# Order of the plain tiles and of the activation sums in two SwiGLU gate stages

## The chip, the cores and the metric

One core of one Trainium2 chip. The metric is the device time of one execution in microseconds, the median over runs. TensorE (PE) multiplies, VectorE (DVE), ScalarE (ACT) and GpSimd (POOL) do the element work, and SyncE (SP) issues most DMA transfers.

## The reference, cut to what matters

```python
def _rmsnorm(x, g):
    xf = x.astype(jnp.float32)
    y = xf * lax.rsqrt(jnp.mean(xf * xf, axis=-1, keepdims=True) + NORM_EPS)
    return (y * g.astype(jnp.float32)).astype(x.dtype)

def _swiglu(h, w_gate, w_up, w_down):
    return (jax.nn.silu(h @ w_gate) * (h @ w_up)) @ w_down
```

The block is a feed-forward net (FFN1), three parallel mixers with an output projection, a second feed-forward net (FFN2) and a final norm. x is 1024 x 1024, the hidden width is 2816, everything is float32. The change touches only the two gate stages, `silu(h @ w_gate) * (h @ w_up)` with h = rmsnorm(x).

## The kernel before, in words

Activations lie transposed: 8 tiles of 128 features (k = 0..7), each in two halves of 512 tokens. Float32 precision is kept by splitting each operand into a high and a low part (`split`, L96 to L102): ScalarE makes the high part (L99), VectorE or GpSimd the low part by a subtraction (L102). Each product is then three matmuls (`mm3`, L119 high x high, L120 high x low of h, L121 low of the weight x high of h).

A gate stage (class `Gates`) has 22 tiles of the hidden width. The first four, f = 0..3, are plain (`plain`, L326): per tile two weights (gate and up, `gu`) in two pieces each, both halves of the tokens, 48 matmuls per half. Tiles 0 and 1 load their weights once for each half. The other 18 are done in pairs by a seven-product block scheme (`run`): h is seen as a 2 x 2 matrix of blocks (k = 0..3 or 4..7, half 0 or 1), and for each k = 0..3 `sums` (L342) forms four combinations t1 to t4 of the four blocks, and splits each: three subtractions on GpSimd (L349, L350, L352), one on VectorE (L351), and then t1, t2, t4, t3. They overwrite the normalized tiles. t4 goes into the slots of h's half 1, k = 0..3, which the plain tiles read last. A weight in flight has one of 4 pairs of high and low tiles (`whi`, `wlo`) and one of 8 raw tiles (`wraw`); the slot comes free with its last reader.

FFN1 starts with the norm still unknown: f = 0, 1 are first run for half 0 on the unnormalized tiles `hu` (scaled by the norm's gain), and `finish` (L308) multiplies by the reciprocal root r afterwards (L313, L323). Meanwhile `step` computes r of both halves and splits the normalized half 1. After that f = 0, 1 run for half 1, then half 0 is normalized (L182) and split, and f = 2, 3 run on both halves.

In FFN2 half 0 of h comes out of the output projection (`wout`) while half 1 is still being projected; the normalized tiles of half 0 are stored to DRAM (`xnd`, L1663), since their ring slots are needed, and loaded back into ring slots (L1711) for the sums after the plain tiles. `rg` is the ring of 10 slots.

The code gives the order of issue; a scheduler then moves instructions ahead within each engine's list as their operands allow. In FFN1 it already draws the sums into the time of the plain tiles. Each engine, and SyncE's DMA queue, works its list strictly in order. In the trace, `h` and `t` are split tiles (one name for high and low), `pgu` a bank of accumulated gate products, `rst` the reciprocal root, `x` half 0 of FFN1's input, `rg` also half 1.

Of the kernel before, what the change touches and what calls it, by code (L numbers as in the profile page):

```python
# [8 lines left out]
FT = mybir.dt.float32  # L9
FR = mybir.dt.float32r  # L10
# [8 lines left out]
KT = 8  # L19
HALF = 512  # L20
# [267 lines left out]
class Gates:  # L288
# [34 lines left out]
            nc.vector.tensor_mul(sg, sg, r)  # L323
        nc.sync.dma_start(self.ad[f][half], sg)

    def plain(self, fs, halves, h, r=lambda: None, loads=None, step=None):  # L326

        B = self.B
        for f in fs:
            w = [[loads.pop(0) if loads else B.wload(self.wgu[f, gu, q], 512) for q in range(2)] for gu in range(2)]  # L330
            for half in halves:
                ps = [self.bank() for _ in range(2)]
                for k in range(KT):
                    wc = slice((k % 4) * 128, (k % 4) * 128 + 128)
                    for gu in range(2):
                        B.mm3(ps[gu], [a[:, wc] for a in w[gu][k // 4]], h[half][k], k == 0, k == KT - 1)
                if step:
                    step()
                for gu in range(2):
                    self.finish(f, half, gu, ps[gu], r())  # L340

    def sums(self, k, raw):  # L342


        B, nc = self.B, self.nc
        a11, a12, a21, a22 = raw
        add = nc.gpsimd
        out = [None] * 4
        add.tensor_sub(a11, a12, a11)  # L349
        add.tensor_sub(a12, a22, a12)  # L350
        nc.vector.tensor_sub(a22, a22, a11)  # L351
        add.tensor_sub(a21, a21, a22)  # L352
        for n, a, eng in ((1, a11, "dve"), (2, a22, "dve"), (4, a21, "pool"), (3, a12, "pool")):
            pool, tag = (B.hp, lambda p: f"h{p}1{k}") if n == 4 else (self.tp, lambda p: f"t{p}{n}{k}")
            t = out[n - 1] = [pool.tile([128, HALF], FR, name=f"t{p}{n}{k}", tag=tag(p)) for p in range(2)]
            B.split(*t, a, eng_lo=eng)
        return out

    def blocks(self, m):

# [1066 lines left out]
def body(ctx, tc, A, VO):  # L1427
    nc = tc.nc
# [44 lines left out]
    with ExitStack() as fs:  # L1473
        with ExitStack() as st:
            B.more_w(fs)
            ring = ring_of(st)
            F = Gates(B, st, ring, A["wgu1"], ad)
            g1 = VO["ffn1_norm"]
            hu, h = ([], []), ([], [])

            def loadx(half, k):
                t = ring() if half else F.tp.tile([128, HALF], FT, name=f"x0{k}", tag=f"t{k // 4}3{k % 4}")
                nc.sync.dma_start(t, A["xT"][k][:, halves[half]])
                return t

            xt, early, acc, r = [[], []], [], [None, None], {}
            for k in range(KT):
                xt[0].append(loadx(0, k))
                if k in LOADS:
                    early.append(B.wload(A["wgu1"][0, LOADS[k][0], LOADS[k][1]], 512))  # L1490
            for k in range(KT):
                xt[1].append(loadx(1, k))
            for k in range(KT):
                B.split_scaled(*B.htile(hu, 0, k), xt[0][k], g1 + k)
                acc[0] = B.add_square(np_, acc[0], xt[0][k], nc.gpsimd)

            def step():
                for half in range(2):
                    if half not in r:
                        r[half] = B.rstd_tiles(np_, nps, xt[1], one) if half else B.rstd(np_, nps, acc[0])  # L1500
                        if half:
                            for k in range(KT):
                                B.normed(xt[1][k], xt[1][k], r[1], g1 + k)
                                B.split(*B.htile(h, 1, k), xt[1][k], eng_lo="pool" if k % 2 else "dve")

            F.plain((0, 1), (0,), hu, lambda: r[0], early, step)
            B.load_consts()
            F.plain((0, 1), (1,), h)
            for k in range(KT):
                B.normed(xt[0][k], xt[0][k], r[0], g1 + k)  # L1510
                B.split(*B.htile(h, 0, k), xt[0][k])
            F.plain((2, 3), (0, 1), h)
            sums = [F.sums(k, (xt[0][k], xt[1][k], xt[0][k + 4], xt[1][k + 4])) for k in range(4)]
            F.run(h, sums)
        mt = met.enter_context(tc.tile_pool(name="met", bufs=1, side="right", reuse_waits="tile"))
        xp = xs.enter_context(tc.tile_pool(name="xp", bufs=1, side="right", reuse_waits="tile"))
# [132 lines left out]
    with ExitStack() as fs:  # L1649
        np_, nps = B.norm_pool(fs)  # L1650
        B.more_w(fs)
        with ExitStack() as st:
# [31 lines left out]
            with tc.tile_pool(name="mgp", bufs=1, reuse_waits="tile") as mp, \  # L1684
# [14 lines left out]
                weave([late(), wout(0, mps)])  # L1699
                weave([wout(1, mps)])  # L1700
            F = Gates(B, st, ring, A["wgu2"], ad)
            F.plain((0, 1), (0,), h, step=lambda: B.tick(4))
            B.drain()
            F.plain((0, 1), (1,), h)
            F.plain((2, 3), (0, 1), h)
            sums = []
            for k in range(4):
                two = []
                for j in (k, k + 4):
                    t = ring()  # L1710
                    nc.sync.dma_start(t, xnd[j])  # L1711
                    two.append(t)
                sums.append(F.sums(k, (two[0], xt[1, k], two[1], xt[1, k + 4])))
            F.run(h, sums)
        xp = fs.enter_context(tc.tile_pool(name="xp2", bufs=1, side="right", reuse_waits="tile"))
        x = [xp.tile([128, S], FT, name=f"x{k}") for k in range(KT)]
# [92 lines left out]
```

## Time and profile before

| | us |
|---|---|
| median of 3 runs | 2962.35 (2958.25 to 2962.57) |
| profiled execution | 2965.43 |
| its span | 2963.4 |
| TensorE busy | 2842.6 (96%) |
| VectorE busy | 1749.2 (59%) |
| ScalarE busy | 1274.8 (43%) |
| GpSimd busy | 636.9 (21%) |

The span is the profiled part of one execution; 2.0 us lie around it. The mean granted clock of TensorE is 0.981 of full speed. FFN1's gate stage begins the program; FFN2's begins at about 2241 us. A busy share is an average over the whole span; what a wait costs is read from the stretch in which it stands.

### The profile page before, as it was taken

What the parts mean: (1) busy time and instruction counts of PE and PEld (TensorE: products, weight loads), DVE (VectorE), ACT (ScalarE), POOL (GpSimd) and SP (SyncE); (2) the same over time, 40 slices, a digit from 0 to 9 for tenths busy, and PEclk for the clock granted to TensorE, in tenths of its full rate; (3) what the DMA queues carried; (4) which work ended last, traced back from release to release, by engine and by line L of the source; (5) the groups of instructions that cost most, each with busy time, mean ns of one, the idle gap of its engine ahead of it and who ended that gap; (6) DMA issues with size and microseconds to landing.
All of it is one profiled execution on the core that took longest, in us unless ns stands there. A gap on an engine that the chain in (4) does not pass through costs nothing. (4 is left out here: it accounts for less than half of the span.)

```text
span 2963.4 us, 39951 instructions
## 1 busy us (share of the span) xinstructions
PE 2842.6 (96%) x13790; PEld 2254.4 (76%) x13790; DVE 1749.2 (59%) x3788; ACT 1274.8 (43%) x2743; POOL 636.9 (21%) x721
## 2 busy tenths in 40 slices
PE   7999999999999999999999889999999799999997
PEld 4788888887887777767767677777787588888886
DVE  8455555627466656666654367888765455555526
ACT  5333333315454345544443356666543233333313
POOL 4422220004011111111110133433321522220002
PEclk8999999999999999999999999999999899999999
DMA  4222226514323212222221642212564222225413
GB/s 150 75 85 86 82 79 202 163 35 148 96 64 87 69 56 72 64 70 73 59 67 57 183 146 80 85 59 69 182 212 140 71 78 83 82 86 191 140 41 105
DMA packets 203046, 294.40 MB, mean 99 GB/s; under 512 B 46131, under 2 KB 75707, under 8 KB 202844
## 3 DMA queue, kind: packets, MB, share of 16 engines
q1 hardware_dynamic: 186384, 263.25, 28.8%
q10 hardware_dynamic: 16460, 28.61, 3.2%
q8 instruction: 108, 1.77, 0.3%
q14 instruction: 94, 0.77, 0.1%
HBM read 223.51 MB, written 68.27 MB: 98 GB/s over the span
## 5 line engine op out<-in xcount | busy, mean ns | idle before, releaser
L99 ACT ACTIVATE whi<-wraw 128x512 fp32r<-128x512 f32 x576 | 345.1, 603 | 755.9 <-PE pgu L120 289.2
L102 DVE TENSOR_TENSOR wlo<-wraw,whi 128x512 fp32r<-128x512 f32 (+1 forms) x568 | 406.4, 719 | 383.0 <-ACT whi L99 343.4
L119 PE MATMUL mm<-h,whi 128*128 128x512 f32 x800 | 329.6, 412 | 0.2 <-ACT gbt L1543 0.2
L121 PE MATMUL mm<-h,wlo 128*128 128x512 f32 x800 | 320.1, 401 | 7.3 <-DVE wlo L102 7.3
L120 PE MATMUL mm<-h,whi 128*128 128x512 f32 x800 | 317.6, 397 | 0.0
L119 PE MATMUL pgu<-h,whi 128*128 128x512 f32 x688 | 273.2, 398 | 15.1 <-ACT whi L99 10.4
L120 PE MATMUL pgu<-h,whi 128*128 128x512 f32 x688 | 274.3, 399 | 8.5 <-DVE h L102 4.5
L121 PE MATMUL pgu<-h,wlo 128*128 128x512 f32 x688 | 274.0, 399 | 7.1 <-DVE wlo L102 7.1
L121 PE MATMUL pd<-a,wlo 128*128 128x512 f32 x704 | 274.3, 390 | 1.7 <-DVE wlo L102 1.7
L119 PE MATMUL pd<-a,whi 128*128 128x512 f32 x704 | 274.0, 389 | 0.6 <-DVE x L256 0.6
L120 PE MATMUL pd<-a,whi 128*128 128x512 f32 x704 | 273.9, 389 | 0.0
L119 PE MATMUL pgu<-t,whi 128*128 128x512 f32 x576 | 225.8, 392 | 8.7 <-ACT t L99 6.6
L120 PE MATMUL pgu<-t,whi 128*128 128x512 f32 x576 | 225.8, 392 | 8.5 <-DVE t L102 8.5
L121 PE MATMUL pgu<-t,wlo 128*128 128x512 f32 x576 | 224.9, 390 | 0.0
L132 POOL TENSOR_TENSOR acc<-acc,sq 128x512 f32<-128x512 f32 x46 | 67.5, 1467 | 579.9 <-ACT sq L131 576.8
L121 PEld LDWEIGHTS mm<-h,wlo 128*128 128x128 f32 x800 | 151.1, 189 | 40.1 <-DVE wlo L102 9.1
L119 PEld LDWEIGHTS mm<-h,whi 128*128 128x128 f32 x800 | 151.3, 189 | 36.1 <-issue 5.3
L120 PEld LDWEIGHTS mm<-h,whi 128*128 128x128 f32 x800 | 151.5, 189 | 28.5 <-issue 3.0
L119 PEld LDWEIGHTS pgu<-h,whi 128*128 128x128 f32 x688 | 131.9, 192 | 45.0 <-ACT whi L99 12.6
L120 PEld LDWEIGHTS pgu<-h,whi 128*128 128x128 f32 x688 | 131.8, 192 | 40.5 <-DVE h L102 6.0
L256 DVE SCALAR_TENSOR_TENSOR x<-pd,x 128x512 f32<-128x512 f32 x128 | 87.7, 687 | 126.2 <-PE pd L121 121.3
L121 PEld LDWEIGHTS pgu<-h,wlo 128*128 128x128 f32 x688 | 131.7, 191 | 38.5 <-DVE wlo L102 11.1
(405 smaller groups left out, 6071.9 us busy)
## 6 DMA issues: line engine op xcount, KB each, us to landing
wraw<-in_wgu SPq DMA_DIRECT2D x192, 256.0 KB, 2.7
wraw<-in_wd SPq DMA_DIRECT2D x96, 256.0 KB, 2.7
ad<-sg SPq DMA_DIRECT2D x88, 256.0 KB, 2.7
wraw<-ad SPq DMA_DIRECT2D x88, 256.0 KB, 2.7
wraw<-in_win SPq DMA_DIRECT2D x52, 256.0 KB, 2.6
wraw<-in_wgb SPq DMA_DIRECT2D x48, 256.0 KB, 2.7
gd<-gbt SPq DMA_DIRECT2D x48, 256.0 KB, 2.0
gbt<-gd ACTq DMA_DIRECT2D x40, 256.0 KB, 2.8
```

The lines of the kernel that those rows point to most:

```text
L99: nc.scalar.activation(hi, src, AF.Copy)
L102: (nc.vector if eng_lo == "dve" else nc.gpsimd).tensor_sub(lo, src, hi.bitcast(FT))
L119: mm(ps, w[0], x[0], start=start, stop=False, **kw)
L120: mm(ps, w[0], x[1], start=False, stop=False, **kw)
L121: mm(ps, w[1], x[0], start=False, stop=stop, **kw)
L132: eng.tensor_add(acc, acc, sq)
L256: nc.vector.scalar_tensor_tensor(x[d][:, c], p, 0.25, x[d][:, c], op0=OP.mult, op1=OP.add)
```

## The change

`sums` makes t1, t2 and t3 only and leaves the fourth, unsplit, in the buffer of its fourth operand. The new `fourth` splits it after the last plain tile. FFN1 runs f = 2 (half 0 on `hu`, half 1 on h) between the two halves of f = 0, 1, and the sums stand ahead of f = 3. FFN2 does the same with h, and its half 0 is loaded back from `xnd` into the slots of the third sum, ahead of the gate stage, instead of into ring slots behind the plain tiles. `r` of `plain` becomes a dictionary from half to reciprocal root.

```diff
--- before.py
+++ after.py
@@ -323,7 +323,7 @@
             nc.vector.tensor_mul(sg, sg, r)
         nc.sync.dma_start(self.ad[f][half], sg)
 
-    def plain(self, fs, halves, h, r=lambda: None, loads=None, step=None):
+    def plain(self, fs, halves, h, r=None, loads=None, step=None):
 
         B = self.B
         for f in fs:
@@ -337,24 +337,31 @@
                 if step:
                     step()
                 for gu in range(2):
-                    self.finish(f, half, gu, ps[gu], r())
+                    self.finish(f, half, gu, ps[gu], r[half] if r and half in r else None)
 
     def sums(self, k, raw):
 
 
-        B, nc = self.B, self.nc
+        nc = self.nc
         a11, a12, a21, a22 = raw
         add = nc.gpsimd
-        out = [None] * 4
+        out = []
         add.tensor_sub(a11, a12, a11)
         add.tensor_sub(a12, a22, a12)
         nc.vector.tensor_sub(a22, a22, a11)
-        add.tensor_sub(a21, a21, a22)
-        for n, a, eng in ((1, a11, "dve"), (2, a22, "dve"), (4, a21, "pool"), (3, a12, "pool")):
-            pool, tag = (B.hp, lambda p: f"h{p}1{k}") if n == 4 else (self.tp, lambda p: f"t{p}{n}{k}")
-            t = out[n - 1] = [pool.tile([128, HALF], FR, name=f"t{p}{n}{k}", tag=tag(p)) for p in range(2)]
-            B.split(*t, a, eng_lo=eng)
-        return out
+        for n, a, eng in ((1, a11, "dve"), (2, a22, "dve"), (3, a12, "pool")):
+            if n == 3:
+                add.tensor_sub(a22, a21, a22)
+            t = [self.tp.tile([128, HALF], FR, name=f"t{p}{n}{k}", tag=f"t{p}{n}{k}") for p in range(2)]
+            self.B.split(*t, a, eng_lo=eng)
+            out.append(t)
+        return out + [a22]
+
+    def fourth(self, k, out):
+
+        t = [self.B.hp.tile([128, HALF], FR, name=f"t{p}4{k}", tag=f"h{p}1{k}") for p in range(2)]
+        self.B.split(*t, out[3], eng_lo="pool" if k % 2 else "dve")
+        out[3] = t
 
     def blocks(self, m):
 
@@ -1503,14 +1510,17 @@
                                 B.normed(xt[1][k], xt[1][k], r[1], g1 + k)
                                 B.split(*B.htile(h, 1, k), xt[1][k], eng_lo="pool" if k % 2 else "dve")
 
-            F.plain((0, 1), (0,), hu, lambda: r[0], early, step)
+            F.plain((0, 1), (0,), hu, r, early, step)
             B.load_consts()
+            F.plain((2,), (0, 1), (hu[0], h[1]), {0: r[0]})
             F.plain((0, 1), (1,), h)
             for k in range(KT):
                 B.normed(xt[0][k], xt[0][k], r[0], g1 + k)
                 B.split(*B.htile(h, 0, k), xt[0][k])
-            F.plain((2, 3), (0, 1), h)
             sums = [F.sums(k, (xt[0][k], xt[1][k], xt[0][k + 4], xt[1][k + 4])) for k in range(4)]
+            F.plain((3,), (0, 1), h)
+            for k in range(4):
+                F.fourth(k, sums[k])
             F.run(h, sums)
         mt = met.enter_context(tc.tile_pool(name="met", bufs=1, side="right", reuse_waits="tile"))
         xp = xs.enter_context(tc.tile_pool(name="xp", bufs=1, side="right", reuse_waits="tile"))
@@ -1699,18 +1709,17 @@
                 weave([late(), wout(0, mps)])
                 weave([wout(1, mps)])
             F = Gates(B, st, ring, A["wgu2"], ad)
+            x0 = [F.tp.tile([128, HALF], FT, name=f"x0{k}", tag=f"t{k // 4}3{k % 4}") for k in range(KT)]
+            for k in range(KT):
+                nc.sync.dma_start(x0[k], xnd[k])
             F.plain((0, 1), (0,), h, step=lambda: B.tick(4))
             B.drain()
+            F.plain((2,), (0, 1), h)
+            sums = [F.sums(k, (x0[k], xt[1, k], x0[k + 4], xt[1, k + 4])) for k in range(4)]
             F.plain((0, 1), (1,), h)
-            F.plain((2, 3), (0, 1), h)
-            sums = []
+            F.plain((3,), (0, 1), h)
             for k in range(4):
-                two = []
-                for j in (k, k + 4):
-                    t = ring()
-                    nc.sync.dma_start(t, xnd[j])
-                    two.append(t)
-                sums.append(F.sums(k, (two[0], xt[1, k], two[1], xt[1, k + 4])))
+                F.fourth(k, sums[k])
             F.run(h, sums)
         xp = fs.enter_context(tc.tile_pool(name="xp2", bufs=1, side="right", reuse_waits="tile"))
         x = [xp.tile([128, S], FT, name=f"x{k}") for k in range(KT)]
```

What the scheduler makes of it, at three places. First, ScalarE in FFN1, where t0nk is the high part of sum n for index k, h0ik that of half i, x0k the normalized half 0, and rg_283 to rg_289 half 1. Before, from the high parts of half 1 on:

```order
L99 ACTIVATE h016_475<-rg_287 128x512
L99 ACTIVATE h017_480<-rg_289 128x512
L99 ACTIVATE whi_660<-wraw_658 128x512
L99 ACTIVATE whi_666<-wraw_664 128x512
L99 ACTIVATE whi_672<-wraw_670 128x512
L316 ACTIVATE rg_652<-pgu_602 128x512
L99 ACTIVATE whi_678<-wraw_676 128x512
L99 ACTIVATE t020_1058<-rg_283 128x512
L99 ACTIVATE t030_1066<-rg_275 128x512
L99 ACTIVATE t021_1078<-rg_285 128x512
L99 ACTIVATE t031_1086<-rg_277 128x512
```

Of the change, from the last high part of half 0 on:

```order
L99 ACTIVATE h007_913<-x07_267 128x512
L99 ACTIVATE t011_936<-x01_243 128x512
L99 ACTIVATE t012_952<-x02_245 128x512
L99 ACTIVATE t013_968<-x03_247 128x512
L99 ACTIVATE whi_725<-wraw_723 128x512
L99 ACTIVATE t020_924<-rg_283 128x512
L99 ACTIVATE whi_731<-wraw_729 128x512
L316 ACTIVATE rg_711<-pgu_661 128x512
L99 ACTIVATE whi_737<-wraw_735 128x512
L99 ACTIVATE t030_929<-rg_275 128x512
L99 ACTIVATE t021_940<-rg_285 128x512
```

The weight pieces of the second tile's pass over half 1 (whi_660 to whi_678) stood ahead of the second and third sums; now those of the first tile's pass (whi_725, whi_731, whi_737) stand behind t010 to t013, and two of them behind t020.

Second, ScalarE in FFN2 at the same step. Before:

```order
L99 ACTIVATE h010_22189<-rg_21674 128x512
L99 ACTIVATE h011_22194<-rg_21732 128x512
L99 ACTIVATE h012_22279<-rg_21788 128x512
L99 ACTIVATE whi_22328<-wraw_22326 128x512
L316 ACT_TABLE_LOAD
L316 ACTIVATE rg_22298<-pgu_22228 128x512
L99 ACTIVATE h013_22284<-rg_21844 128x512
```

Of the change:

```order
L99 ACTIVATE h010_22208<-rg_21677 128x512
L99 ACTIVATE t010_22472<-x00_22102 128x512
L99 ACTIVATE h011_22213<-rg_21735 128x512
L99 ACTIVATE h012_22298<-rg_21791 128x512
L99 ACTIVATE t011_22488<-x01_22103 128x512
L99 ACTIVATE t012_22504<-x02_22104 128x512
L99 ACTIVATE whi_22347<-wraw_22345 128x512
L316 ACT_TABLE_LOAD
L316 ACTIVATE rg_22317<-pgu_22247 128x512
L99 ACTIVATE h013_22303<-rg_21847 128x512
```

t010, t011 and t012 now stand between the high parts of half 1 and ahead of a weight's high part (whi_22347, the third tile's up weight; at this step before, whi_22328).

Third, SyncE's queue at the end of the output projection, with the stores of xnd and the first gate weights (in_wgu2). Before:

```order
L1663 DMA xnd4_207<-rg_21324 128x512
L1679 DMA x2d2_197<-rg_21788 128x512
L1663 DMA xnd5_208<-rg_21397 128x512
L106 DMA wraw_22099<-in_wgu2 128x512
L106 DMA wraw_22105<-in_wgu2 128x512
L1663 DMA xnd6_209<-rg_21470 128x512
L1679 DMA x2d3_198<-rg_21844 128x512
L1663 DMA xnd7_210<-rg_21543 128x512
L106 DMA wraw_22111<-in_wgu2 128x512
```

Of the change:

```order
L1673 DMA xnd5_208<-rg_21400 128x512
L1714 DMA x02_22104<-xnd2_205 128x512
L1714 DMA x03_22105<-xnd3_206 128x512
L1714 DMA x04_22106<-xnd4_207 128x512
L1673 DMA xnd6_209<-rg_21473 128x512
L1689 DMA x2d3_198<-rg_21847 128x512
L1673 DMA xnd7_210<-rg_21546 128x512
L1714 DMA x05_22107<-xnd5_208 128x512
L1714 DMA x06_22108<-xnd6_209 128x512
L106 DMA wraw_22118<-in_wgu2 128x512
L1714 DMA x07_22109<-xnd7_210 128x512
L1689 DMA x2d4_199<-rg_21903 128x512
```

The reloads x00 to x07 stand between the stores; the first gate weight (wraw_22118, before wraw_22099) comes behind the seventh reload, the second behind the eighth.

## Rows read from the trace of the kernel before

**Rows 1.** The stretches view, two undisturbed stretches; its columns in the first line
```profile
core 0: us, PE busy (x) PEld busy (x) DVE busy (x) ACT busy (x) POOL busy (x), PEclk, DMA share, GB/s
100.00:120.00 20.00, 20.00 (x90) 16.57 (x89) 4.49 (x7) 2.90 (x5) 2.57 (x2) 1.00 0.24 80
2400.00:2440.00 40.00, 40.00 (x178) 33.14 (x177) 21.20 (x30) 15.26 (x26) 11.66 (x9) 1.00 0.26 80
```

**Rows 2.** The stretches view, first gate stage
```profile
60.00:80.00 20.00, 12.35 (x43) 8.58 (x42) 20.00 (x22) 6.14 (x12) 12.88 (x8) 0.87 0.23 66
45.35:100.00 54.65, 40.72 (x150) 30.71 (x150) 43.91 (x49) 21.25 (x36) 31.32 (x19) 0.84 0.21 63
```

**Rows 3.** The stretches view, second gate stage
```profile
2338.00:2376.00 38.00, 19.44 (x50) 12.00 (x49) 22.89 (x18) 13.06 (x22) 31.88 (x22) 0.69 0.22 69
2264.40:2400.00 135.60, 114.81 (x466) 89.44 (x464) 63.91 (x80) 41.31 (x71) 50.05 (x35) 0.91 0.26 81
```

**Rows 4.** The timeline of TensorE, first gate stage: start, length, instruction, [idle before <-releaser]
```profile
49.30 1.22 PE L119 MATMUL pgu<-h,whi 128*128 128x512 f32 x2 [3.83 <-ACT h L99]
...
62.78 0.50 PE L120 MATMUL pgu<-h,whi 128*128 128x512 f32 x1 [1.91 <-DVE h L102]
...
76.64 0.80 PE L121 MATMUL pgu<-h,wlo 128*128 128x512 f32 x1 [4.22 <-DVE wlo L102]
```

**Rows 5.** The timeline of VectorE, both gate stages
```profile
46.64 0.68 DVE L170 SCALAR_TENSOR_TENSOR rst<-nu,rst 128x512 f32<-128x512 f32 x1
...
55.90 5.16 DVE L182 SCALAR_TENSOR_TENSOR rg<-rg,vec,rst 128x512 f32<-128x512 f32 x3
...
2263.30 2.74 DVE L182 SCALAR_TENSOR_TENSOR rg<-rg,vec,rst 128x512 f32<-128x512 f32 x4
```

**Rows 6.** The timeline of GpSimd, both gate stages
```profile
48.73 5.01 POOL L349 TENSOR_TENSOR x<-rg,x 128x512 f32<-128x512 f32 x3 [28.81 <-DVE rg L182]
...
2293.98 1.29 POOL L367 TENSOR_TENSOR wS<-wraw 128x512 f32<-128x512 f32 x1 [55.88 <-DMA wraw<-in_wgu]
```

**Rows 7.** The timeline of TensorE, second gate stage
```profile
2343.45 0.80 PE L119 MATMUL pgu<-h,whi 128*128 128x512 f32 x1 [3.25 <-ACT whi L99]
...
2347.56 0.62 PE L121 MATMUL pgu<-h,wlo 128*128 128x512 f32 x1
2347.99 0.43 PE L119 MATMUL pgu<-t,whi 128*128 128x512 f32 x1
...
2353.08 0.50 PE L120 MATMUL pgu<-t,whi 128*128 128x512 f32 x1 [2.29 <-DVE t L102]
...
2363.62 0.79 PE L119 MATMUL pgu<-t,whi 128*128 128x512 f32 x1 [5.15 <-ACT t L99]
...
2370.05 0.80 PE L120 MATMUL pgu<-t,whi 128*128 128x512 f32 x1 [1.71 <-DVE t L102]
```

**Rows 8.** The timeline of ScalarE, second gate stage
```profile
2342.25 0.63 ACT L99 ACTIVATE t<-rg 128x512 fp32r<-128x512 f32 x1 [2.77 <-POOL rg L352]
```

**Rows 9.** The timeline of SyncE's queue, second gate stage
```profile
2328.20 5.99 SPq L1711 DMA_DIRECT2D rg<-xnd  x2
```

**Rows 10.** The timeline of SyncE's queue, output projection
```profile
2208.60 5.16 SPq L1663 DMA_DIRECT2D xnd<-rg  x4
...
2219.01 1.54 SPq L106 DMA_DIRECT2D wraw<-in_wgu  x2
2220.84 0.33 SPq L1663 DMA_DIRECT2D xnd<-rg  x1
```

**Rows 11.** The transfers view, 2195 to 2245: line, count, KB each, median us to landing
```profile
wraw<-in_wgu SPq DMA_DIRECT2D x12, 256.0 KB, 3.8
...
xnd<-rg SPq DMA_DIRECT2D x8, 256.0 KB, 4.3
```

**Rows 12.** The timeline of ScalarE, output projection
```profile
2232.35 0.63 ACT L99 ACTIVATE whi<-wraw 128x512 fp32r<-128x512 f32 x1 [1.12 <-PE wo L120]
```

**Rows 13.** The chain of waits that ended last, 2195 to 2270: start, length, what
```profile
2211.57 3.63 DMA rg<-x1d
```

**Rows 14.** The timeline of TensorE, begin of the second gate stage
```profile
2241.52 0.47 PE L119 MATMUL pgu<-h,whi 128*128 128x512 f32 x1 [0.88 <-DVE rg L1678]
```

## The prediction

> **What bounds the kernel now.** I read the shares of busy time on the page first: TensorE works nearly the whole span, so only the places where it waits or runs at its lower clock can give time back. Next I cut the two gate stages into stretches. Undisturbed, a stretch of 40 us holds 178 matmuls at a granted clock of 1.00, so one matmul costs 40/178 = 0.2247 us [rows 1]. With that price every other stretch can be weighed. In the first gate stage, 45.35 to 100 holds only 150 matmuls, at 0.84 [rows 2]: 150 x 0.2247 = 33.7 us of work in 54.65 us, so 20.9 us are lost. In the second, 2264.40 to 2400 holds 466 [rows 3]: 104.7 us of work in 135.60 us, so 30.9 us are lost, and most of it lies between 2338 and 2376, where 38 us hold 50 matmuls (11.2 us of work) at a clock of 0.69 [rows 3]. The two losses together, 51.8 us, are all that the change can win.
>
> The timelines say who is late. In the first stage TensorE waits for the halves of h, then for a weight's low part [rows 4]. VectorE is behind both: it is busy for 20.00 of the 20 us from 60 to 80 [rows 2], and its operations on two SBUF tiles take 5.16/3 = 1.72 us each while GpSimd makes sums, against 2.74/4 = 0.68 us at a time when GpSimd rests [rows 5]. GpSimd's own take 5.01/3 = 1.67 us there and 1.29 us alone [rows 6]. In the second stage the sums come last: TensorE waits 3.25, 2.29 and 5.15 us for a weight's high part and for t [rows 7], since ScalarE's conversions wait for GpSimd in their turn [rows 8]. The sums are late because the reload of half 0 starts only at 2328.20 [rows 9]. Until then GpSimd does almost nothing in this stage: it had been idle for 55.88 us at 2293.98 [rows 6].
>
> **First gate stage.** The third tile's half 0 now runs on the unnormalized h, so TensorE has 24 of its matmuls and 2 of the next bank, then 20 on half 1 (the order), where it stood still before. ScalarE no longer converts half 0 ahead of the reciprocal root of half 1, whose last step began at 46.64 [rows 5]; I put its end at 43.5, an estimate. What remains is VectorE's list, counted in the order of the change:
> - The low part of the third tile's up weight (first piece) is the 15th instruction from the first norm. Four of the 15 meet a GpSimd split (about 1.70 each), eleven take about 0.66: 14.1 us, so 57.6, and 1.1 more for the hand-overs, an estimate: 58.7. TensorE gets there 46 matmuls after 45.35, at 55.7. Stall 3.0.
> - The high part behind t020 on ScalarE (whi_731, the up weight of the first tile's second pass; the first order piece) comes 17 VectorE instructions later, eight of them beside a GpSimd sum: 8 x 1.72 + 9 x 0.66 = 19.7 us after 58.7, so 78.4. TensorE arrives at 72.8 (53 matmuls, and 2.2 of slow clock). Stall 5.6; the low part behind it could make it 7.3.
> - The up weight of the second tile's second pass waits behind conversions of the third sums in the same way: 2.2, by the same count.
> - The clock: after the 3.25 us wait, TensorE ran at the lower rate from 2343.45 to 2347.99 [rows 7], with starts 0.43 us apart (2347.56 to 2347.99); some 11 such matmuls cost 11 x 0.2 = 2.2 us. I charge it twice here, after the first and the second stall. After 2.29 us it kept its rate [rows 7].
>
> That is 3.0 + 5.6 + 2.2 + 4.4 = 15.2 us lost against 20.9: **gain 5.7**. Its bounds are 2 (each stall at its upper end) and 12 (no clock charge and a second stall of half the size).
>
> **Second gate stage.** The sums now start with the norms of half 1, at about 2260. GpSimd's cover is its idle time [rows 6]; VectorE pays for it. The low part of the third tile's gate weight (second piece) is the 19th VectorE instruction from 2259.5, eight of them now in company: 8 x 1.70 + 11 x 0.61 = 20.3, so 2279.8. TensorE can do 33 matmuls (7.4 us) after 2264.4 and has by then waited 1.5, 2.2 and 0.5 us for operands behind t010 to t012 on ScalarE and behind the paired norms (the second order piece): 2276.0, so a stall of 3.8, and 2.2 for the clock. One more of 1.4 comes with the up weight of the first tile's second pass. Sum 11.6 against 30.9: **gain 19.3**. The sums are done near 2298, some 40 us ahead of the hole at 2338, so the hole goes. The fourth sum's conversions wait for the last plain tile, but 72 matmuls (16.2 us) stand between it and their reader, and four ScalarE conversions of 0.63 us and two splits each on VectorE and GpSimd need under 6 us: nothing. Bounds 13 (each stall doubled but the last, both clocks slow) and 27 (only the 3.8 stays).
>
> **The reload.** Eight transfers of 256 KB move from 2328 and later to the time of the output projection, and stand in SP's queue between the stores that they read. A store of xnd lands 4.3 us after issue [rows 11]; the seventh store was issued at 2220.84 [rows 10], so the seventh reload can go at 2225.1, and the first gate weight behind it (the third order piece) at 2225.5 instead of 2219.01 [rows 10]. With 3.8 us to land [rows 11] it is there at 2229.3; ScalarE wants it at 2232.35 [rows 12]. Cover 3.0 us, so the queue costs nothing. The traffic may slow the read of x1d on the chain, 3.63 us long [rows 13]: between nothing and that once more; nearest to the row, I take **-0.7**, a fifth of it.
>
> **Sum.** 5.7 + 19.3 - 0.7 = 24.3. The profiled execution took 2965.43 us (its span of 2963.4 and 2.0 around it), which gives 2941.1; the median of the runs is 3.1 lower, hence **2938**.
>
> Whether paired operations cost more than I charge is open: three in a row give 1.70 per pair [rows 5, 6], less than 0.68 + 1.29 = 1.97. The Trainium skill ("SBUF — State Buffer", section "Who interferes with whom") has the loser of the shared port fully blocked, which would make it 1.97, and the 20 pairs counted above 5.4 us dearer: 2943. The rows decide for 1.70.
>
> **The rivals.**
> - (a) The first stage gains nothing: its hole only moves to the ScalarE conversions behind t020. For: VectorE has the same operations and is already without idle time. Against: 48 matmuls that need no norm. Gain 19.3 - 0.7, so 2944.
> - (b) The reload makes the gate weights late. If each reload waits for one store's full round, seven rounds of 4.3 from 2212.9 end at 2243.0, and the first weight, landed and split, comes at 2248.1 for a TensorE that wants it at 2241.5 [rows 14]; the second one a round later: 6.6 + 4.3 = 10.9 lost, 2949. For: SP's queue is strictly in order. Against: the stores were issued spread out, so most have landed when their reload's turn comes. It decides once the first weight is issued after 2228.5.
> - (c) More cover than I counted: half of what I left as loss, 15.2 + 11.6 = 26.8 us, goes too. Gain 24.3 + 13.4 = 37.7, so 2925. For: my stalls rest on VectorE's list being strictly serial. Against: they follow from counts of instructions.
> - (d) Slower: the clock does not come back between the new, shorter stalls. Then about 83 matmuls of the first stage and 80 of the second run with starts 0.2 us further apart: 17 + 16 = 33 us, more than the gain of 24.3, and 2938 + 33 = 2971. It decides when over 121 matmuls run slow (24.3/0.2). For: after the 5.15 us wait TensorE was still slow behind a wait of 1.71 us at 2370.05 [rows 7]. Against: it was back 4.5 us after 2343.45 and then kept its rate through 2.29 us [rows 7]. The Trainium skill ("TensorE: Matmul & The Clock Gate", section "HAM oscillation — how this bites in real kernels") says that a kernel with a wait in every round starts each round cold; by that rule this is the case to fear, and the trace agrees only in part.
> - That the change does not do what it says I can exclude for the order of instructions: the sums do stand ahead.
>
> **How the numbers follow.** Chances: the forecast 0.53, (a) 0.14, (b) 0.12, (c) 0.12, (d) 0.04, and 0.05 for (a) and (b) together, which leaves 24.3 - 5.7 - 10.9 = 7.7, and 1.4 at the lower bound of the second stage. A measurement of this kernel tells 0.2% (5.9 us) from no change. Faster: 0.53 + 0.14 + 0.12 + 0.12 = 0.91; the 0.05 counts as the same; slower 0.04. The range runs from 2925 (c) to 2951 (b and its spread), which leaves out (d), the double case and the outer part of (b) and (c).
>
> **What would show it.** Right: in the second stage no stretch of 38 us with 50 matmuls; the stage's 466 matmuls take about 116 us; GpSimd makes sums from about 2260; the reload's rows lie between 2212 and 2227 and the first gate weight is issued near 2225.5. In the first stage, 150 matmuls in about 49 us, with the longest wait near 73 for a weight's high part on ScalarE. Wrong: a granted clock under 0.8 over more than 25 us in either stage, TensorE waiting for weights near 2242, or a new wait of over 5 us between 2265 and 2300.

## The result, and the profile after

| | before | after |
|---|---|---|
| median, us | 2962.57 (5 runs) | 2942.34 (5 runs, 2937.98 to 2950.77) |
| profiled execution, us | 2965.43 | 2942.52 |
| its span, us | 2963.4 | 2940.7 |
| mean granted clock | 0.981 | 0.986 |

The ratio after to before is 0.9929 (95% interval 0.9904 to 0.9953), a gain of 14 to 28 us. The median lies 4.3 us above the forecast of 2938, inside its range; the profiled execution, on which the sum was made, took 2942.52 against the 2941.1 of the sum.

First the two gate stages in the stretches view of the changed kernel (columns as in [rows 1]). The second stage's stretch has the length of that before and begins 1.94 us earlier, as the stage itself does:

```profile
45.35:100.00 54.65, 41.47 (x166) 32.47 (x165) 50.45 (x53) 24.34 (x43) 33.51 (x21) 0.91 0.23 67
2262.46:2398.06 135.60, 129.29 (x552) 105.28 (x551) 77.23 (x99) 49.12 (x84) 54.19 (x35) 0.97 0.25 76
```

In the second stage 552 matmuls stand where 466 did [rows 3]: 552 x 0.2247 = 124.0 us of work in 135.60, so 11.6 us are lost, which is the figure of the sum. In the first, 166 against 150 [rows 2]: 17.3 us lost, against 15.2 in the sum.

TensorE's timeline of the changed kernel, first stage: the rows with long waits.

```profile
58.22 0.50 PE L121 MATMUL pgu<-h,wlo 128*128 128x512 f32 x1 [2.70 <-DVE wlo L102]
...
77.72 0.80 PE L119 MATMUL pgu<-h,whi 128*128 128x512 f32 x1 [7.19 <-ACT whi L99]
...
92.99 0.50 PE L119 MATMUL pgu<-h,whi 128*128 128x512 f32 x1 [2.75 <-ACT whi L99]
...
94.26 0.79 PE L121 MATMUL pgu<-h,wlo 128*128 128x512 f32 x1 [0.53 <-DVE wlo L102]
```

The first wait ends at 58.22, after 2.70 us; the forecast had 3.0, with its end at 58.7. The second ends at 77.72 after 7.19 us, for a weight's high part on ScalarE; the forecast had it end at 78.4, with 5.6 us and 7.3 as its upper end. The third, with the low part behind it, is 2.75 + 0.53 us where 2.2 was put.

ScalarE's timeline shows why, in the same stage:

```profile
71.96 0.61 ACT L99 ACTIVATE whi<-wraw 128x512 fp32r<-128x512 f32 x1
76.52 0.63 ACT L99 ACTIVATE t<-rg 128x512 fp32r<-128x512 f32 x1 [3.94 <-DVE rg L351]
77.05 0.61 ACT L99 ACTIVATE whi<-wraw 128x512 fp32r<-128x512 f32 x1
```

The weight's high part at 77.05 (whi_731 of the order) had to stand behind a conversion of the second sum, which waited for VectorE's L351 to 76.52. And VectorE, in its timeline, came to that subtraction late (the first two rows are the first norms and the low part that the first wait was for):

```profile
44.91 3.39 DVE L182 SCALAR_TENSOR_TENSOR rg<-rg,vec,rst 128x512 f32<-128x512 f32 x5
...
57.01 1.15 DVE L102 TENSOR_TENSOR wlo<-wraw,whi 128x512 fp32r<-128x512 f32 x1
...
60.49 1.28 DVE L102 TENSOR_TENSOR h<-x,h 128x512 fp32r<-128x512 f32 x2
...
63.40 3.47 DVE L102 TENSOR_TENSOR h<-x,h 128x512 fp32r<-128x512 f32 x2
...
70.19 3.42 DVE L102 TENSOR_TENSOR h<-x,h 128x512 fp32r<-128x512 f32 x2
73.53 1.74 DVE L102 TENSOR_TENSOR wlo<-wraw,whi 128x512 fp32r<-128x512 f32 x1
```

Two subtractions begun before GpSimd's first sum took 1.28 us; two beside its sums 3.47, and another two 3.42 us.

TensorE in the second stage of the changed kernel:

```profile
2264.73 0.50 PE L119 MATMUL pgu<-h,whi 128*128 128x512 f32 x1 [1.96 <-ACT whi L99]
...
2272.83 0.50 PE L120 MATMUL pgu<-h,whi 128*128 128x512 f32 x1 [0.52 <-DVE h L102]
...
2278.12 0.50 PE L121 MATMUL pgu<-h,wlo 128*128 128x512 f32 x1 [3.53 <-DVE wlo L102]
```

The wait predicted for the third tile's low part (3.8 us, ending at 2279.8 on the clock of before) is there: 3.53 us, ending at 2278.12, which is 2280.06 when the 1.94 us are added back.

The reload, in SyncE's queue, the transfers view and the two engines that might have waited:

```profile
2206.32 2.69 SPq L1673 DMA_DIRECT2D xnd<-rg  x3
2209.11 1.75 SPq L1714 DMA_DIRECT2D x<-xnd  x2
...
2221.09 4.16 SPq L1714 DMA_DIRECT2D x<-xnd  x2
2225.34 0.38 SPq L106 DMA_DIRECT2D wraw<-in_wgu  x1
```

```profile
wraw<-in_wgu SPq DMA_DIRECT2D x12, 256.0 KB, 5.7
...
x<-xnd SPq DMA_DIRECT2D x8, 256.0 KB, 5.4
```

```profile
2238.57 0.63 ACT L99 ACTIVATE whi<-wraw 128x512 fp32r<-128x512 f32 x1 [2.09 <-DMA wraw<-in_wgu]
```

```profile
2239.58 0.47 PE L119 MATMUL pgu<-h,whi 128*128 128x512 f32 x1 [0.88 <-DVE rg L1688]
```

The reloads (`x<-xnd`) run between the stores, and the first gate weight is issued at 2225.34, 1.8 us later than forecast once the shift of 1.94 us is added back. The weights land in a median of 5.7 us instead of 3.8 [rows 11]. One conversion, at 2238.57, was released by a transfer rather than by TensorE, yet it stands where it stood relative to the stage (at 2240.51 before, 1.94 us later), and TensorE begins the stage after the same 0.88 us wait as before [rows 14]. The cover held, with nothing left over.

To compare kernels part by part, two marks of each profile are used below: the first matmul of the first net's down projection (L119, `pd<-a,whi`), which ends the first gate stage, and the time from the second stage's first `pgu` matmul to the second net's first `pd` matmul.

| profile of | first stage ends | second stage takes | the part between |
|---|---|---|---|
| before | 475.73 | 462.17 | 1765.79 |
| after | 471.52 | 442.64 | 1768.06 |

So the first stage gained 4.2 us (forecast 5.7) and the second 19.5 (forecast 19.3). The part between (the mixers and projections) has as many instructions on every engine in both, and in the changed kernel the transfers of the reload besides; over all profiles of this study it took 1764.0 to 1772.3 us. A median carries that spread. The second mark doesn't; the first has a spread of its own, told with e1 and e2. Behind the second stage the changed kernel takes another 1.2 us less (258.5 against 259.7).

### The profile page after: what moved, and what is told of

It is laid out like the page before. It is cut to its first block, busy times and chain, and to the rows that moved or that the text cites. A ratio compares the mean times of both kernels' runs of the same rounds, so it can differ in the third digit from the quotient of the medians.

```text
span 2940.7 us, 39952 instructions
## 1 busy us (share of the span) xinstructions
PE 2836.4 (96%) x13790; PEld 2252.7 (77%) x13790; DVE 1755.4 (60%) x3794; ACT 1276.1 (43%) x2743; POOL 638.0 (22%) x717
## 5 line engine op out<-in xcount | busy, mean ns | idle before, releaser
L119 PE MATMUL mm<-h,whi 128*128 128x512 f32 x800 | 330.1, 413 | 0.2 <-ACT gbt L1553 0.2
L119 PE MATMUL pgu<-h,whi 128*128 128x512 f32 x688 | 272.5, 396 | 19.5 <-ACT whi L99 18.6
L119 PE MATMUL pd<-a,whi 128*128 128x512 f32 x704 | 273.9, 389 | 0.0
L119 PE MATMUL pgu<-t,whi 128*128 128x512 f32 x576 | 224.3, 389 | 2.1 <-ACT rg L412 2.1
L119 PEld LDWEIGHTS mm<-h,whi 128*128 128x128 f32 x800 | 151.8, 190 | 36.4 <-issue 5.3
L119 PEld LDWEIGHTS pgu<-h,whi 128*128 128x128 f32 x688 | 131.5, 191 | 49.4 <-ACT whi L99 21.6
L121 PEld LDWEIGHTS pd<-a,wlo 128*128 128x128 f32 x704 | 132.2, 188 | 30.4 <-DVE wlo L102 3.0
```

What stands on the lines that cost most here:

```text
L119: mm(ps, w[0], x[0], start=start, stop=False, **kw)
L121: mm(ps, w[1], x[0], start=False, stop=stop, **kw)
```

## The experiments

All are read by the two marks; where a median was taken, it stands with its interval.

### The two stages apart

e1 is the changed kernel with the second stage as before (its sums make t4 at once again), e2 with the first as before:

```diff
--- changed, second stage
+++ e1
-            F.plain((2,), (0, 1), h)
-            sums = [F.sums(k, (x0[k], xt[1, k], x0[k + 4], xt[1, k + 4])) for k in range(4)]
             F.plain((0, 1), (1,), h)
-            F.plain((3,), (0, 1), h)
+            F.plain((2, 3), (0, 1), h)
...
+                    t = ring()
+                    nc.sync.dma_start(t, xnd[j])
--- changed, first stage
+++ e2
-            F.plain((2,), (0, 1), (hu[0], h[1]), {0: r[0]})
             F.plain((0, 1), (1,), h)
...
-            F.plain((3,), (0, 1), h)
+            F.plain((2, 3), (0, 1), h)
```

> The first gate stage as changed, the second as before. If the two stages are worth what their own traces show and do not touch each other: first down-projection matmul of the first net near 471.5 us (475.73 before, 471.52 changed), second gate stage 462 us from its first to the down-projection's first matmul (462.17 before, 442.64 changed), median 2 to 4 us under the kernel before. Rival, the first stage's gain is lost again in the mixers whatever is done behind it (2.3 of 4.2 us were gone by 2241): no difference in the median within 1.5 us, although the first stage ends 4 us earlier.

> The second gate stage as changed, the first as before. If the stages are independent: first down-projection matmul of the first net near 475.7 us, second gate stage near 442.6 us, median 17 to 21 us under the kernel before (about 2943 to 2945). Rival, part of the second stage's gain rests on the first one's edits: second stage over 447 us.

Measured: e1 471.92 and 462.53 us, median 2960.72 against 2965.97, ratio 0.9979 (0.9967 to 0.9992). e2 474.18 and 442.58 us, median 2943.85, ratio 0.9923 (0.9899 to 0.9948). The stages are independent: each changed stage keeps its own number to 0.4 us. The first stage's mark is less steady (474.18, 475.73 and, in e3 below, 476.59 for the same code of that stage; 471.52 and 471.92 for the changed one), so its gain lies between 2.3 and 5.1 us. That the gain is lost again in the mixers falls: e1 keeps it in the median (2 to 10 us; the medians differ by 5.2, more than the 2 to 4 expected).

### The reload alone, and the third tile put back

e3 is the kernel before with the early reload and nothing else:

```diff
+            x0 = [F.tp.tile([128, HALF], FT, name=f"x0{k}", tag=f"t{k // 4}3{k % 4}") for k in range(KT)]
+            for k in range(KT):
+                nc.sync.dma_start(x0[k], xnd[k])
             F.plain((0, 1), (0,), h, step=lambda: B.tick(4))
             B.drain()
             F.plain((0, 1), (1,), h)
             F.plain((2, 3), (0, 1), h)
-            sums = []
...
+            sums = [F.sums(k, (x0[k], xt[1, k], x0[k + 4], xt[1, k + 4])) for k in range(4)]
             F.run(h, sums)
```

> The kernel before with one edit: half 0 is reloaded ahead of the second gate stage into the slots of the third sum; sums, fourth sum and third tile stand in the text as before. Theory A, the late reload alone made the hole, and the scheduler draws the first three sums ahead by itself once their operand is there (its lists do): second gate stage 441 to 448 us, median 14 to 21 us under the kernel before. Theory B, the place of the sums and of the third tile in the text matters too, as the third tile's 48 matmuls per half cover the norms: second stage 449 to 458 us, 4 to 13 us gained. Theory C, the hole only moves: over 459 us.

Measured: second stage 447.17 us, median 2951.91, ratio 0.9943 (0.9926 to 0.9960). Theory A: 15.0 of the 19.5 us come from the reload alone. The sums stand behind all plain tiles in the text, and run ahead of them all the same: GpSimd's first L349 is at 2261.87, 18.9 us after the stage begins, as in the changed kernel. Two waits and VectorE's list in e3:

```profile
2276.19 0.79 PE L120 MATMUL pgu<-h,whi 128*128 128x512 f32 x1 [5.09 <-DVE h L102]
...
2281.48 0.80 PE L121 MATMUL pgu<-h,wlo 128*128 128x512 f32 x1 [2.36 <-DVE wlo L102]
```

```profile
2280.74 2.48 DVE L102 TENSOR_TENSOR wlo<-wraw,whi 128x512 fp32r<-128x512 f32 x4
2283.15 0.68 DVE L351 TENSOR_TENSOR rg<-rg,x 128x512 f32<-128x512 f32 x1
```

The wait of 5.09 us, 33.2 us after the stage begins, is what the third tile covers: in the changed kernel the wait for a low part of h at the same place, 2272.83, is 0.52 us.

e5 is the changed kernel with the third tile back in its place (second stage shown; the first likewise):

```diff
             B.drain()
-            F.plain((2,), (0, 1), h)
             sums = [F.sums(k, (x0[k], xt[1, k], x0[k + 4], xt[1, k + 4])) for k in range(4)]
             F.plain((0, 1), (1,), h)
-            F.plain((3,), (0, 1), h)
+            F.plain((2, 3), (0, 1), h)
```

> The changed kernel with the third tile put back behind the first two in both stages; reload, sums and fourth sum as changed. Theory A, the third tile between the halves gives the first stage its 4.2 us (it covers the norm of half 1) and the second stage nothing: first down-projection matmul near 475.7 us, second gate stage 441 to 445 us. Theory B, it is half of the second stage's gain as well: second stage 449 us or more. Theory C, the sums' place gives the first stage its gain: first down-projection matmul under 473 us.

Measured (one execution, of 2962.83): first stage ends at 475.46, within the spread of the kernel before, so theory A for the first stage: without the third tile nothing is gained there. The second stage takes 454.97 us, theory B, and a surprise beyond it: this is 7.8 us more than the reload alone. The stretches view of the same 20 us of the stage, e5, whose stage begins 4.73 us later, and then e3:

```profile
2284.73:2304.73 20.00, 11.30 (x35) 8.53 (x35) 12.00 (x20) 6.97 (x12) 16.38 (x8) 0.62 0.24 79
```

```profile
2280.00:2300.00 20.00, 18.40 (x67) 14.60 (x68) 16.26 (x25) 7.92 (x14) 7.40 (x4) 0.81 0.43 120
```

35 matmuls against 67. In e5 TensorE waits here, and VectorE's timeline shows what is ahead:

```profile
2293.43 1.40 PE L121 MATMUL pgu<-h,wlo 128*128 128x512 f32 x2 [9.58 <-DVE wlo L102]
```

```profile
2291.50 0.67 DVE L102 TENSOR_TENSOR t<-x,t 128x512 fp32r<-128x512 f32 x1
2292.10 0.67 DVE L102 TENSOR_TENSOR t<-rg,t 128x512 fp32r<-128x512 f32 x1
2292.70 2.48 DVE L102 TENSOR_TENSOR wlo<-wraw,whi 128x512 fp32r<-128x512 f32 x4
```

Four low parts of weights, one of which TensorE waits 9.58 us for, come behind the subtractions of the sums; in e3 the four stand ahead of the first L351 (2280.74, above), and the wait is 2.36 us. Written ahead of the plain tiles' second half, the sums have precedence over its weights in the lists; with the third tile between, the weights that TensorE needs meanwhile stand ahead of the sums again (in the changed kernel three low parts of weights are made at 2277.39, and the first L351 after them at 2279.20). e5 differs from e3 in the fourth sum too, which no run has by itself; the rows put the time on the order of the four low parts.

### The sums written last

```diff
-            sums = [F.sums(k, (x0[k], xt[1, k], x0[k + 4], xt[1, k + 4])) for k in range(4)]
             F.plain((0, 1), (1,), h)
             F.plain((3,), (0, 1), h)
+            sums = [F.sums(k, (x0[k], xt[1, k], x0[k + 4], xt[1, k + 4])) for k in range(4)]
```

(the same in the first stage)

> The changed kernel with the sums written behind the last plain tile again in both stages; reload, third tile and fourth sum as changed. Theory A, the place of the sums in the text does nothing once their operands are there, as the scheduler draws them ahead and its lists are nearly the same: second gate stage 441 to 445 us, first down-projection matmul near 471.5. Theory B, it counts as it does with the third tile put back (447.2 with the reload alone, 455.0 with the sums written ahead too): the conversions yield to the weights and the second stage is 434 to 440 us. Theory C, the sums come later and the hole comes back in part: over 447.

Measured: 472.52 and 444.04 us, one execution of 2944.90. Theory A, within 1.4 us. Given the reload and the third tile, the place of the sums in the text, which the change names first, does next to nothing.

### The element work on VectorE instead of GpSimd

e4 is the changed kernel with this:

```diff
-        add = nc.gpsimd
+        add = nc.vector
-        for n, a, eng in ((1, a11, "dve"), (2, a22, "dve"), (3, a12, "pool")):
+        for n, a, eng in ((1, a11, "dve"), (2, a22, "dve"), (3, a12, "dve")):
-        self.B.split(*t, out[3], eng_lo="pool" if k % 2 else "dve")
+        self.B.split(*t, out[3])
-                                B.split(*B.htile(h, 1, k), xt[1][k], eng_lo="pool" if k % 2 else "dve")
+                                B.split(*B.htile(h, 1, k), xt[1][k])
```

> The changed kernel with the sums' subtractions, the third and fourth sum's low parts and all low parts of half 1 on VectorE; GpSimd does none of them. Theory A, in these stretches VectorE is what comes last, and an operation on GpSimd costs it more (1.70 us for a pair against 0.68 alone) than doing the work itself (0.61 more): the low part waited for at 58 us comes 17 instructions after the norms' start, near 54, the high part waited for at 78 near 64, both before TensorE wants them. First down-projection matmul of the first net 457 to 464 us (471.5 changed), second gate stage 431 to 438 us (442.6 changed), median 13 to 25 us under the changed kernel, 2917 to 2929. Theory B, VectorE only gets a longer list (28 instructions more in each stage, 17 us): first matmul at 471 or later, second stage 443 or longer, median 2942 or more.

Measured: 456.61 and 437.70 us, median 2922.25 (2917.24 to 2927.86), ratio to before 0.9857 (0.9834 to 0.9880). Theory A, with the first stage 0.4 us better than its range; the interval lies clear of the changed kernel's. The first stage in the stretches view, and VectorE's timeline:

```profile
45.35:100.00 54.65, 52.92 (x233) 43.28 (x232) 50.35 (x80) 27.04 (x47) 9.70 (x4) 1.00 0.30 92
```

```profile
48.59 3.10 DVE L102 TENSOR_TENSOR h<-rg,h 128x512 fp32r<-128x512 f32 x5
...
56.58 0.69 DVE L102 TENSOR_TENSOR wlo<-wraw,whi 128x512 fp32r<-128x512 f32 x1
...
65.65 0.69 DVE L102 TENSOR_TENSOR wlo<-wraw,whi 128x512 fp32r<-128x512 f32 x1
```

233 matmuls at full clock, where the changed kernel has 166: 2.3 us lost. Five low parts of h take 3.10 us with no partner, and the low parts of the two weights that TensorE had waited for to 58.22 and to 77.72 are begun at 56.58 and 65.65. The waits of 2.70 and 7.19 us are gone. The first low part came 2.6 us later than the expected 54; 1.8 of it is that the norms began at 45.28 rather than at 43.5. The expectation's count was too high: 22 operations move in the first stage and 18 in the second, not 28.

e6 makes the same exchange in the kernel before, and nothing else:

```diff
-        add = nc.gpsimd
+        add = nc.vector
-        for n, a, eng in ((1, a11, "dve"), (2, a22, "dve"), (4, a21, "pool"), (3, a12, "pool")):
+        for n, a, eng in ((1, a11, "dve"), (2, a22, "dve"), (4, a21, "dve"), (3, a12, "dve")):
-                                B.split(*B.htile(h, 1, k), xt[1][k], eng_lo="pool" if k % 2 else "dve")
+                                B.split(*B.htile(h, 1, k), xt[1][k])
```

> The kernel before, with the same work moved from GpSimd to VectorE and nothing else. Theory A (paired operations are the cost, in the old order too): first down-projection matmul of the first net 463 to 470 us (475.73 before); second stage 450 to 457 us (462.17 before), since GpSimd was busy for 31.88 of the 38 us of the hole with operations that take 0.61 on VectorE; the reload stays late, so the hole does not vanish. Theory B (order and reload are all): 474 to 477, and 460 to 464.

Measured: 462.13 and 453.74 us, median 2941.65, ratio 0.9922 (0.9905 to 0.9939): the whole gain of the change under study, without moving a tile. Theory A, 0.9 us better than its range in the first stage. The stretches of [rows 2] in e6, that of the hole [rows 3] moved by the 15.27 us that this stage begins earlier, and TensorE in what is left of it:

```profile
60.00:80.00 20.00, 20.00 (x89) 16.23 (x88) 19.89 (x34) 9.01 (x16) 0.00 (x0) 1.00 0.45 139
45.35:100.00 54.65, 50.77 (x212) 40.71 (x211) 44.08 (x71) 24.61 (x42) 7.83 (x3) 0.94 0.27 83
2322.73:2360.73 38.00, 29.47 (x94) 19.98 (x93) 30.73 (x47) 17.92 (x31) 5.84 (x4) 0.82 0.24 76
```

```profile
2328.30 0.80 PE L121 MATMUL pgu<-h,wlo 128*128 128x512 f32 x1 [1.70 <-DVE wlo L102]
...
2334.65 0.50 PE L119 MATMUL pgu<-t,whi 128*128 128x512 f32 x1 [1.55 <-ACT rg L405]
```

60 to 80 holds 89 matmuls where 43 stood; VectorE is busy throughout in both. The 38 us of the hole hold 94 matmuls instead of 50, and what remains are waits of up to 1.7 us. From 60 to 80 in the first stage VectorE had no idle time before, so what it was spared is what counts. In the hole it was busy for 22.89 of the 38 us and GpSimd for 31.88 [rows 3]; there the exchange also shortens GpSimd's own chain of sums, and how much of the 8.4 us gained in the second stage comes from that was not tried apart.

e9 adds the early reload to e6:

```diff
+            x0 = [F.tp.tile([128, HALF], FT, name=f"x0{k}", tag=f"t{k // 4}3{k % 4}") for k in range(KT)]
+            for k in range(KT):
+                nc.sync.dma_start(x0[k], xnd[k])
```

> The kernel before with two edits: the early reload (447.17 us for the second stage by itself) and the sums' and half 1's element work on VectorE (453.74 by itself). First stage as with VectorE alone: first down-projection matmul near 462. Theory A, with unpaired operations the place of the third tile and of the sums is worth nothing in the second stage: 434 to 439 us (437.70 for the changed kernel on VectorE), median 2925 to 2932, the rest of its distance to 2922 being the first stage's 5.5 us. Theory B, the third tile is still needed to cover the norms: 441 to 446 us, median 2933 to 2940.

Measured: 459.50 and 436.78 us, median 2925.27, ratio 0.9862 (0.9846 to 0.9879). Theory A: with the element work on VectorE, the second stage needs neither the third tile between nor the sums ahead. Its first stage has the code of e6, and its mark (459.50 against 462.13) shows the spread once more. The longest wait of the second stage's plain tiles is this one:

```profile
2259.04 0.50 PE L121 MATMUL pgu<-h,wlo 128*128 128x512 f32 x1 [1.33 <-DVE wlo L102]
```

e10 moves only the four low parts of the first stage's half 1 to VectorE, in the changed kernel:

```diff
-                                B.split(*B.htile(h, 1, k), xt[1][k], eng_lo="pool" if k % 2 else "dve")
+                                B.split(*B.htile(h, 1, k), xt[1][k])
```

> The changed kernel with only the four low parts of the first stage's half 1 (odd k) moved from GpSimd to VectorE; sums stay on GpSimd, second stage untouched (442 to 444 us). Theory A, the pairs on the list ahead of a weight are what TensorE waits for: the wait of 2.7 us at 58 goes (the low part comes 18 unpaired instructions after the norms' start), the wait of 7.2 us at 78 shrinks to 0 to 3, as the high part now stands behind only two conversions of sums, and a wait of 2 to 5 us is left behind the second and third sums: first down-projection matmul 459 to 465. Theory B, GpSimd's sums as such are the bound, wherever the splits are made: the wait near 78 stays over 5 us, 468 to 472.

Measured: first stage ends at 463.55, second stage 442.62, one execution of 2933.41. Theory A: 8.0 of the 14.9 us that e4 wins in the first stage come from these four operations. TensorE's waits:

```profile
69.16 0.50 PE L119 MATMUL pgu<-h,whi 128*128 128x512 f32 x1 [0.80 <-ACT whi L99]
...
85.67 0.80 PE L119 MATMUL pgu<-h,whi 128*128 128x512 f32 x1 [3.69 <-ACT whi L99]
```

The wait at 58 is gone, the one of 7.19 us is 0.80, and one of 3.69 stays: ScalarE makes the weight's high part at 85.00, behind three conversions of sums from 83.26 on, the first of which waited for VectorE's L351.

## Why the prediction was right

- **Second stage, 19.3 forecast, 19.5 measured.** The count of VectorE's list with eight paired operations gave the main wait within 0.3 us of its place and its length. TensorE came to it at 2274.59 (2276.53 with the shift added back), where 2276.0 was forecast, though the waits ahead of it, put at 1.5, 2.2 and 0.5, were 1.96, 0.52 and 0.07: a slow stretch took the rest. e2, with the same second stage, had no slow stretch there, and waits of 1.96 and 2.12; the second ends 33.2 us after the stage begins in both, and the stage takes 442.58 and 442.64 us. So this slow stretch, ahead of a wait whose end VectorE sets, only filled that wait. Behind the main wait 2.2 for the clock and 1.4 for one more wait were put; a slow stretch of 8 matmuls (about 1.6 us) and a wait of 0.23 stand there. That the sum is met to a tenth is luck among these. e3 shows which part carries the gain: the early reload, 15.0 us. The working named the late reload as what held the sums back, but priced it together with the rest; the place of the sums in the text is not what makes them start (e7), their operand is.
- **First stage, 5.7 forecast, 4.2 measured** (2.3 to 5.1 with the spread of the mark). The first two waits end within 0.7 us of their forecast places. For the first, two errors offset each other: the norms began at 44.91 and not at 43.5, and the 15 instructions from there on took 13.25 us where 15.2 had been put. The mis-sized term is the stall behind t020: 7.19 us, near the upper end, instead of 5.6. VectorE's list ended it where forecast, 0.7 us early; TensorE came to it at 70.53 instead of 72.8, as the slow clock charged ahead of it did not come. The third wait was 3.3 instead of 2.2. e5 and e7 show the third tile to carry this gain: without it the mark is at 475.46, with it and the sums written last at 472.52. e10 shows that the paired operations decide the rest.
- **The clock.** The 4.4 us charged in the first stage had the right size: of the 17.3 us lost, the waits take 13.2, which leaves 4.2, some 3 of it in 13 slow matmuls. The place was right only for one of the two charges. The granted clock is 1.00 from 58.22 to 70.53, behind the 2.70 us wait; it is 0.50, the lower of the two levels, from 77.72 to 80.50 behind the 7.19 us wait, and from 94.26 to 97.40 behind the waits of 2.75 and 0.53. In the second stage there were two slow stretches of 8 matmuls, after 1.96 and 3.53 us, where one was charged.
- **The reload, 0.7 charged.** TensorE begins the stage after the same wait, and the output projection (first `wo` matmul to the stage) took 118.56 us against 119.01. Over the eight profiles with the early reload it took 116.5 to 123.9 us, over the three without 118.7 to 119.6, so a cost of 0.7 can be neither seen nor excluded. Transfers became slower (reads of x1d land in a median of 5.6 us instead of 4.6), but the chain's piece of [rows 13] is 3.70 us instead of 3.63. Rival (b) was right that the first weight goes out later, but with the shift added back it went at 2227.28, short of the 2228.5 at which (b) decides.
- **Rival (a)**, that the first stage gains nothing, falls by 2.3 to 5.1 us, though its mechanism, the conversions behind t020, is the longest wait of the stage. **Rival (c)** falls: no half of the forecast loss went; 17.3 and 11.6 us stayed where 15.2 and 11.6 were put. What the remaining waits rest on is the paired operations (e4), which no rival named: 20 us more lay in the choice of engine, as much as in the order. **Rival (d)** falls: the granted clock of the first stage is 0.91, and 0.97 in the second.
- **1.70 us for a pair.** Two VectorE subtractions beside GpSimd took 3.47, another two 3.42 us, so 1.72 each. The dearer 1.97 is not borne out in these stretches.

What stays open: why the part between the stages varies by 8 us from one profile to the next, and which of the 22 and 18 operations that e4 moves matter most beyond the four of e10; they were not tried one by one, and in the second stage not parted into what VectorE is spared and what GpSimd's own chain loses.

## What to carry to other kernels

Where VectorE is the engine that comes last, count what an operation on GpSimd costs it: here 1.0 us more for each VectorE operation that met one, and doing the work on VectorE itself costs 0.6. Before moving work in time, ask what its operand waits for: one early reload gave three quarters of what the whole change gave in that stage, since the scheduler drew the rest ahead by itself. And work written ahead of a stage takes precedence over that stage's own weights; it needs cover of its own (the third tile), or it costs time (e5).

## What the runs showed of the hardware that was not expected

Pairs of VectorE and GpSimd operations did not always alternate. GpSimd and then VectorE, changed kernel, second stage:

```profile
2258.43 5.07 POOL L349 TENSOR_TENSOR x<-rg,x 128x512 f32<-128x512 f32 x3 [22.28 <-issue]
...
2281.76 5.90 POOL L354 TENSOR_TENSOR rg<-x,rg 128x512 f32<-128x512 f32 x1 [7.24 <-ACT t L99]
2287.74 1.29 POOL L102 TENSOR_TENSOR t<-rg,t 128x512 fp32r<-128x512 f32 x1
```

```profile
2281.61 0.68 DVE L102 TENSOR_TENSOR t<-x,t 128x512 fp32r<-128x512 f32 x1
2282.21 0.68 DVE L102 TENSOR_TENSOR t<-rg,t 128x512 fp32r<-128x512 f32 x1
2282.81 0.68 DVE L351 TENSOR_TENSOR rg<-rg,x 128x512 f32<-128x512 f32 x1
...
2287.27 0.69 DVE L318 SCALAR_TENSOR_TENSOR sg<-rg,pgu 128x512 f32<-128x512 f32 x1 [0.76 <-ACT rg L316]
```

One subtraction on GpSimd spans 5.90 us (1.29 alone, 1.7 in a pair) while VectorE goes through its own at the unpaired pace, starts 0.60 us apart; it ends 1.16 us after VectorE's last one, behind which VectorE has a gap of 0.76 us. In e5 the same subtraction spans 8.28 us and in e10 7.08 us, and both end 1.14 us after the last of VectorE's run; in e10 VectorE had no gap there, but went on with L318, which takes one operand from a bank of gate products (`pgu`). That is about the length of the subtraction alone (1.29), so GpSimd seems to have got no turn until VectorE's run of such operations broke off; in the stretches counted above the two took turns. The Trainium skill ("SBUF — State Buffer", section "Who interferes with whom") says that the side which comes second fully blocks and that the order of issue decides who that is. This row agrees with the blocking; it does not show why the turns differ between the two stretches.

The clock does not follow the wait alone. The changed kernel and e2 have the same second stage, and both wait 1.96 us there, 25.2 us after it begins. The stretches of 3.72 us from the end of that wait, changed kernel and e2:

```profile
2264.73:2268.45 3.72, 3.72 (x10) 2.90 (x11) 3.72 (x4) 3.52 (x5) 3.06 (x2) 0.55 0.00 0
```

```profile
2265.08:2268.80 3.72, 3.72 (x16) 3.10 (x17) 3.72 (x4) 3.53 (x5) 3.06 (x2) 1.00 0.00 0
```

10 matmuls near the lower level in the one, 16 at full clock in the other. The kernel before and e9 differ likewise after the same three waits (0.49, 0.40 and 1.34 us, the last to 2270.95; 0.49, 0.41 and 1.33, to 2259.04): the granted clock of the 5.05 us behind is 1.00 in the one and 0.66 in the other. So what TensorE did since the stage began does not say whether the clock falls, and no run here shows what does. Where it fell in these stretches, 8 matmuls ran with starts about 0.2 us further apart, some 1.6 us.
